# Nearest-neighbour upsampling: a first block of rows with its own partition layout, and a first store that waits for the second load

## The chip, the cores and the metric

The kernel runs on one core of a Trainium2 chip. Its engines run side by side and meet through semaphores: here VectorE (DVE in the profile) and ScalarE (ACT) copy within the on-chip memory, and SyncE (SP) issues the transfers, which 16 DMA engines carry out. The on-chip memory has 128 partitions. The metric is the device time of one execution in microseconds; the median of the runs counts.

## The reference

```python
def setup_inputs():
    batch, channels, h, w = (16, 64, 64, 64)
    return {'x': np.random.randn(batch, channels, h, w).astype(np.float32), 'scale_factor': 2}

def reference(x, scale_factor):
    batch, channels, h, w = x.shape
    new_h, new_w = (h * scale_factor, w * scale_factor)
    result = np.zeros((batch, channels, new_h, new_w), dtype=np.float32)
    for i in range(new_h):
        for j in range(new_w):
            result[:, :, i, j] = x[:, :, i // scale_factor, j // scale_factor].copy()
    return result.astype(np.float32)
```

Every element of x becomes a 2 x 2 square of the output. x has 65,536 rows of 64 floats (16.8 MB); each row becomes two output rows of 128 floats, 1 KB together (67.1 MB in all). Nothing is calculated: the kernel moves data.

## The kernel before

**Layout.** All rows of x are numbered through, and partition p owns rows 512p to 512p + 511 (`xp`, `op`). So a transfer of rows lo to hi takes one contiguous piece of memory per partition; the pieces of neighbouring partitions are 128 KiB apart in x and 512 KiB apart in the output.

**On-chip memory.** One tile `mem` holds, per partition, `FREE` = 79 rows' worth of output space (`WF` floats) and behind it all 512 rows of x (`xt`). An expanded chunk is written there too: chunks with an even number at offset 0, those with an odd number ending just below the first row of x that is still unread (line 208), so they lie partly over rows of x that are used up. Two chunks in a row never overlap, and every chunk overlaps the one before last. A copy into a chunk's place therefore waits until the store of the chunk before last has been read out and landed.

**Loads.** Three, cut at rows 0, 32, 288 and 512 (lines 192 to 195). All three are issued on SP one after the other, ahead of the barrier at the program's start (`begin_before_barrier` moves SP's first three instructions there; it needs them to have no waits).

**Chunks.** The loop at line 204 goes over nine chunks of `rows`. In each, VectorE expands the first `kv` rows (line 213) and ScalarE the others (line 214): the operand `expanded` reads each element twice for the columns and each row twice. In the first chunk ScalarE has one row only, in the others VectorE has 9/16. When both are done, SP issues the chunk's store (line 215). SP works in order: a store that waits holds all later ones back. All transfers share SP's one DMA queue.

**The end.** `close_early` arranges the waits and the clearing of semaphores behind the last store.

Of the kernel before, what the change touches and what calls it, by code (L numbers as in the profile page):

```python
# [153 lines left out]
@with_exitstack  # L154
def kernel(
    ctx: ExitStack,
    tc: tile.TileContext,
    x: bass.AP,
    scale_factor: int,
    out: bass.AP,  # L160
):
    nc = tc.nc
    nc.at_finalize(begin_before_barrier)
    nc.at_finalize(close_early)
    P = nc.NUM_PARTITIONS
    s = int(scale_factor)
    B, C, H, W = x.shape
    R = B * C * H // P
    fdt = x.dtype

    xp = x.rearrange("b c h w -> (b c h) w").rearrange("(p r) w -> p r w", p=P)
    op = out.rearrange("b c (h hd) w -> (b c h) (hd w)", hd=s).rearrange(
        "(p r) w -> p r w", p=P
    )

    rows = [54, 38, 52, 63, 52, 64, 63, 63, 63]
    GROW = s * s
    FREE = 79
    WF = FREE * GROW * W
    assert sum(rows) == R
    mem_pool = ctx.enter_context(tc.tile_pool(name="mem", bufs=1))
    mem = mem_pool.tile([P, WF + R * W], fdt, name="mem")
    xt = mem[:, WF:].rearrange("p (r w) -> p r w", r=R)

    HEAD = 32
    cuts = [0, HEAD, R // 2 + HEAD, R]
    for lo, hi in zip(cuts, cuts[1:]):
        nc.sync.dma_start(out=xt[:, lo:hi], in_=xp[:, lo:hi])  # L195

    def expanded(r0, r1):
        return (
            xt[:, r0:r1].unsqueeze(2).unsqueeze(4).to_broadcast([P, r1 - r0, s, W, s])
        )  # L200

    r0 = 0
    before = (0, 0)
    for n, k in enumerate(rows):
        size = k * GROW * W
        at = 0 if n % 2 == 0 else WF + r0 * W - size
        assert at >= before[1] or at + size <= before[0]
        before = (at, at + size)
        u = mem[:, at : at + size].rearrange(
            "p (k a w b) -> p k a w b", k=k, a=s, w=W  # L210
        )
        kv = k - 1 if n == 0 else k * 9 // 16
        nc.vector.tensor_copy(out=u[:, :kv], in_=expanded(r0, r0 + kv))  # L213
        nc.scalar.copy(out=u[:, kv:], in_=expanded(r0 + kv, r0 + k))  # L214
        nc.sync.dma_start(out=op[:, r0 : r0 + k, :], in_=u)  # L215
        r0 += k


# [33 lines left out]
```

## Time and profile before

| | |
|---|---|
| time, median of 3 runs | 197.24 us (196.97 to 197.29) |
| the profiled execution's own span | 195.86 us |
| VectorE busy | 78.6 us, 40% |
| ScalarE busy | 46.5 us, 24% |
| bytes moved | 83.89 MB, 428 GB/s over the span |
| DMA packets | 1728: for each of 12 transfers one per partition, and 16 for the semaphore |
| loads land (slowest engine) | 4.76, 24.10, 41.04 us |
| first store issued, landed | 38.57, 57.37 us |
| last store issued, landed | 167.3, 195.83 us |

The span goes from the first to the last instruction of the profiled execution; what lies around it, 1.38 us against the median, is the start and the end of the program. Times in the text are microseconds from the start of the span. A transfer is told by three moments: its issue on SP, the start and end of its packets on each DMA engine, and its landing, when the last of the 16 engines has raised the semaphore. In the groups of instructions, 128x8960 stands for 128 partitions with 8960 elements each: one row of x is 256 output elements, so that is 35 rows.

### The profile page before, as it was taken

What the parts mean: (1) busy time and instruction counts of PE and PEld (TensorE: products, weight loads), DVE (VectorE), ACT (ScalarE), POOL (GpSimd) and SP (SyncE); (2) the same over time, 40 slices, a digit from 0 to 9 for tenths busy, and PEclk for the clock granted to TensorE, in tenths of its full rate; (3) what the DMA queues carried; (4) which work ended last, traced back from release to release, by engine and by line L of the source; (5) the groups of instructions that cost most, each with busy time, mean ns of one, the idle gap of its engine ahead of it and who ended that gap; (6) DMA issues with size and microseconds to landing.
All of it is one profiled execution on the core that took longest, in us unless ns stands there. A gap on an engine that the chain in (4) does not pass through costs nothing.

```text
span 195.9 us, 102 instructions
## 1 busy us (share of the span) xinstructions
DVE 78.6 (40%) x9; ACT 46.5 (24%) x10; POOL 0.2 (0%) x4
## 2 busy tenths in 40 slices
DVE  0000099990029399078008106930692079100000
ACT  2000000160027093074910006665000074000000
POOL 0000000000000000000000000000000000000000
DMA  9999989889899989899999899999999999999994
GB/s 428 428 428 428 402 375 550 386 361 542 361 435 397 540 348 522 348 422 422 448 417 500 370 500 428 428 428 428 422 422 422 435 435 514 461 435 448 435 422 211
DMA packets 1728, 83.89 MB, mean 428 GB/s; under 512 B 192, under 2 KB 192, under 8 KB 192
## 3 DMA queue, kind: packets, MB, share of 16 engines
q1 hardware_dynamic: 1728, 83.89, 99.2%
HBM read 16.78 MB, written 67.11 MB: 428 GB/s over the span
## 4 chain that ended last, share of the span: by engine, by line
DMA 60%; DVE 25%; issue 0%; SPq 0%; DVEq 0%
DMA out_dram<-mem 48%; DVE mem L213 25%; DMA mem<-in_x_dram 12%; SPq L195 0%; DVEq L213 0%; SPq L215 0%
## 5 line engine op out<-in xcount | busy, mean ns | idle before, releaser
L213 DVE COPY mem<-mem 128x8960 f32<-128x8960 f32 (+4 forms) x9 | 78.6, 8745 | 88.7 <-DMA out_dram<-mem 64.5
L214 ACT COPY mem<-mem 128x7168 f32<-128x7168 f32 (+3 forms) x9 | 45.2, 5027 | 115.6 <-DMA out_dram<-mem 74.1
L214 ACT ACT_TABLE_LOAD x1 | 1.3, 1283 | 1.7 <-PEq L233 1.7
L233 POOL MEMSET const-uint8-127<- 128x1 uint8 x1 | 0.1, 102 | 0.0
L233 POOL MEMSET const-bfloat16-1.0<- 128x1 bf16 x1 | 0.1, 101 | 0.0
L233 POOL MEMSET const-float32-0.0<- 128x1 f32 x1 | 0.1, 98 | 0.2 <-issue 0.2
L233 POOL MEMSET const-float32-1.0<- 128x1 f32 x1 | 0.1, 98 | 0.0
## 6 DMA issues: line engine op xcount, KB each, us to landing
out_dram<-mem SPq DMA_DIRECT2D x4, 8064.0 KB, 28.5
out_dram<-mem SPq DMA_DIRECT2D x2, 6656.0 KB, 22.9
mem<-in_x_dram SPq DMA_DIRECT2D x1, 7168.0 KB, 40.1
out_dram<-mem SPq DMA_DIRECT2D x1, 6912.0 KB, 18.8
out_dram<-mem SPq DMA_DIRECT2D x1, 4864.0 KB, 24.7
mem<-in_x_dram SPq DMA_DIRECT2D x1, 1024.0 KB, 4.8
mem<-in_x_dram SPq DMA_DIRECT2D x1, 23.7
out_dram<-mem SPq DMA_DIRECT2D x1, 30.0
```

What stands on the lines that cost most here:

```text
L213: nc.vector.tensor_copy(out=u[:, :kv], in_=expanded(r0, r0 + kv))
L214: nc.scalar.copy(out=u[:, kv:], in_=expanded(r0 + kv, r0 + k))
L233: nc = _bacc.Bacc("TRN2", target_bir_lowering=False, num_devices=1)
```

## The change

The rows of x are dealt out in two blocks. Of the first 128 x 61 rows, partition p owns rows 61p to 61p + 60; of the remaining 128 x 451, it owns 451 consecutive ones. `of_partitions` gives the piece of x or of the output that holds rows lo to hi of every partition. The pieces of neighbouring partitions are now 15.25 KiB apart in the first load and 61 KiB in the first store, 112.75 and 451 KiB in the others.

The loads are cut at rows 0, 61, 480 and 512. The first load is what the first store needs; the last has 32 rows, 8 KB per partition. The chunks are 61, 33, 52, 63, 52, 63, 63, 63 and 62 rows (before: 54, 38, 52, 63, 52, 64, 63, 63, 63). VectorE's part of each chunk but the first falls from 9/16 to 7/16. The first store gets a wait for the second load's semaphore, besides the waits for its two copies.

```diff
-    xp = x.rearrange("b c h w -> (b c h) w").rearrange("(p r) w -> p r w", p=P)
-    op = out.rearrange("b c (h hd) w -> (b c h) (hd w)", hd=s).rearrange(
-        "(p r) w -> p r w", p=P
-    )
-    rows = [54, 38, 52, 63, 52, 64, 63, 63, 63]
+    FIRST = 61
+    xr = x.rearrange("b c h w -> (b c h) w")
+    orow = out.rearrange("b c (h hd) w -> (b c h) (hd w)", hd=s)
+    blocks = ((0, FIRST), (FIRST, R))
+
+    def of_partitions(t, lo, hi):
+        b0, b1 = next(b for b in blocks if b[0] <= lo and hi <= b[1])
+        whole = t[P * b0 : P * b1].rearrange("(p r) w -> p r w", p=P)
+        return whole[:, lo - b0 : hi - b0]
+
+    rows = [61, 33, 52, 63, 52, 63, 63, 63, 62]
...
-    HEAD = 32
-    cuts = [0, HEAD, R // 2 + HEAD, R]
-    for lo, hi in zip(cuts, cuts[1:]):
-        nc.sync.dma_start(out=xt[:, lo:hi], in_=xp[:, lo:hi])
+    cuts = [0, FIRST, R - 32, R]
+    loads = [
+        nc.sync.dma_start(out=xt[:, lo:hi], in_=of_partitions(xr, lo, hi))
+        for lo, hi in zip(cuts, cuts[1:])
+    ]
...
-        kv = k - 1 if n == 0 else k * 9 // 16
+        kv = k - 1 if n == 0 else k * 7 // 16
         nc.vector.tensor_copy(out=u[:, :kv], in_=expanded(r0, r0 + kv))
         nc.scalar.copy(out=u[:, kv:], in_=expanded(r0 + kv, r0 + k))
-        nc.sync.dma_start(out=op[:, r0 : r0 + k, :], in_=u)
+        store = nc.sync.dma_start(out=of_partitions(orow, r0, r0 + k), in_=u)
+        if n == 0:
+            tc.add_manual_dep(
+                store.ins,
+                loads[1].ins.name,
+                mybir.DependencyInfo(
+                    mybir.DependencyClass.Sync, mybir.DependencyReason.DATA
+                ),
+                reason="the first store goes behind the second load",
+            )
         r0 += k
```

## The prediction

> **What bounds the kernel now.** I read the page first, for which resource is full.
>
> ```profile
> span 195.9 us, 102 instructions
> ...
> DVE 0000099990029399078008106930692079100000
> ...
> DMA  9999989889899989899999899999999999999994
> ...
> q1 hardware_dynamic: 1728, 83.89, 99.2%
> ```
>
> The DMA engines are busy for 99.2% of the span, VectorE for 40%. 0.8% of 195.86 us is 1.6 us: that is all that lies outside packets. Next I read the chain of waits, to see where the copies touch the end.
>
> ```profile
> 0.43 23.67 DMA mem<-in_x_dram
> ...
> 24.20 14.30 DVE mem L213
> ...
> 38.57 18.80 DMA out_dram<-mem
> ...
> 57.46 7.90 DVE mem L213
> ...
> 65.43 19.09 DMA out_dram<-mem
> ```
>
> The chain alternates between copies and transfers, but this is only the order in which buffers come free: while a copy of the chain runs, the queue still has another transfer. So a faster copy gains nothing until the queue runs dry, and a slower one costs only from there. How near that is, the packet records of the trace (start, duration, size of each) show. Within an engine a packet normally starts 6 ns after the one before. The only gaps in the middle of the run are at the first store: it is issued at 38.57, the loads' packets end between 40.05 and 40.65 on the different engines, and three engines that ended at 40.21 to 40.24 got their first store packet only at 40.33 to 40.36. These three waited 0.13 us each; the slowest engine, which sets the end, did not wait.
>
> Third, the stretches, for the rate.
>
> ```profile
> 1.00:2.00 1.00, 0.00 (x0) 0.27 (x1) 0.00 (x0) 1.00 1.04 238
> 2.00:3.00 1.00, 0.00 (x0) 1.00 (x1) 0.00 (x0) 1.00 0.98 410
> 5.00:10.00 5.00, 0.00 (x0) 0.00 (x0) 0.00 (x0) 1.00 0.97 419
> 60.00:190.00 130.00, 56.14 (x7) 38.41 (x7) 0.00 (x0) 1.00 1.00 432
> ```
>
> The last column is GB/s, a packet's bytes counted at its end. Loads alone and stores alone run at the same rate; only the first microsecond of data is slow. The packet records agree: 64 KB load and store packets together take 2418.7 ns, 63 KB store packets 2381.4, 38 KB ones 1440.4. The line through the first and the last of these is 37.63 ns per KB and 10.6 ns per packet. One partition-row of a store (1 KB, eight partitions per engine) is thus 0.302 us and of a load 0.076: 512 rows are 154.8 and 38.7 us, 193.5 in all. The rest of the span is 1.01 us from the first issue to the first packet, 0.50 us per engine of slow first packets (29 of the 128 packets of 8 KB are over 320 ns where the others take 309), 0.36 us from the last packet to its landing, and engines that are 0.6 us apart from the first load on (they landed it at 4.16 to 4.76, and the last store at 195.08 to 195.83).
>
> **The change part by part.** Bytes stay, so 193.5 us stay.
>
> *Loads.* Three as before, issued in the same places, of 61, 419 and 32 rows. The second holds 419 x 256 = 107,264 bytes per partition, and no packet of this trace exceeds 65,536. Cut in two it makes 8 packets more per engine: 8 x 10.6 ns = +0.085 us on the path. Bounds: nothing if it stays whole; many small pieces is a rival. The Trainium skill, "DMA: Bandwidth & Descriptors", section "Why a DMA increments its semaphore by 16 and not by 1", implies that a contiguous row over 64 KiB must be cut and becomes many tiny pieces only where no divisor fits; 26,816 floats halve, which by that rule is the +0.085. No run here shows such a row yet.
>
> *The start.* The first packets are 15.25 KB instead of 8 and 15.25 KB apart in memory instead of 128. Bounds: the 0.50 us of slow packets goes (-0.50), or doubles with the packets' size (+0.50). I take -0.1: the slow packets all end before 2.7 us, as if it were a matter of time and not of bytes, and the rate at the end is that of the slowest engine, whose start (spread over 1.01 to 1.40) stays.
>
> *First copy.* It needs the first load alone: 29 rows more than before, 4.76 + 29 x 0.076 = landed at 7.0. VectorE has 60 rows. Among the nine VectorE groups one stands out:
>
> ```profile
> L213 DVE COPY mem<-mem 128x8960 f32<-128x8960 f32 x4 | 37.9, 9486 | 33.9 <-DMA out_dram<-mem 33.9
> L213 DVE COPY mem<-mem 128x13568 f32<-128x13568 f32 x1 | 14.3, 14286 | 24.2 <-DMA mem<-in_x_dram 24.2
> L213 DVE COPY mem<-mem 128x9216 f32<-128x9216 f32 x1 | 5.0, 4961 | 11.1 <-DMA out_dram<-mem 11.1
> L214 ACT COPY mem<-mem 128x7168 f32<-128x7168 f32 x5 | 30.8, 6165 | 56.1 <-DMA out_dram<-mem 49.7 <-DVE mem L213 6.4
> L214 ACT COPY mem<-mem 128x256 f32<-128x256 f32 x1 | 0.4, 405 | 21.1 <-DMA mem<-in_x_dram 21.1
> ```
>
> 36 rows (9216 elements) take 0.54 ns per element, all others, of an odd number of rows, 1.05. So 60 rows are 8.3 us by the even row, 16.2 by the odd: done at 15 to 23, hidden by the loads either way, with 15 us of cover.
>
> *The hold.* The first store waits on SP for the second load. The loads end as before plus 0.085. The last one is 8 packets x 309 ns + 9 ns for the semaphore = 2.48 us per engine, so the second lands at 41.04 (the loads' last landing) - 2.48 + 0.085 = 38.65, and 0.07 later (copy end 38.50 to issue 38.57 now) the store is issued: 38.72 against 38.57. From issue to the end of the loads on the slowest engine it is 40.65 + 0.085 - 38.72 = 2.02 us, now 2.08. The three late engines show 1.76 to 1.79 us from issue to a first store packet. So the slowest engine keeps 0.2 us, while the engines ahead wait some 0.1 to 0.3 us, which they have. Cost on the path 0; bounds 0 and 0.06 (if the slowest engine now has no slack). If the last load gave no cover at all: 0.36 + 0.07 + 1.79 = 2.2 us. Behind the held store on SP are only the other stores, and the next one's copies cannot begin before the second load either. Without the hold the store would queue behind all loads, so holding it moves no packet forward.
>
> *Second store.* 33 rows, 14 on VectorE, 19 on ScalarE. ScalarE's two rows above give 0.833 ns per element and 0.19 us: 4864 elements are 4.2 us, issue at 43.0, behind a first store that lasts until 59.
>
> *Third store.* It waits for the first store's buffer: landing at 57.37 + 7 rows x 0.302 + 0.085 = 59.6. ScalarE's 30 rows are 6.6 us, issue at 66.3, first packet by 68.1. The second store's 33 rows keep the fastest engine until 59.6 - 0.96 (landing delay and spread) + 10.0 = 68.6. Cover left 0.5 us on the fastest engine, 1.1 on the slowest; now it is 0.6 on the fastest (65.43 + 1.79 against 67.85). If ScalarE took over 1.1 us longer, the excess would count.
>
> *Later copies.* At 7/16, 27 rows on VectorE are 7.4 us, 36 on ScalarE 7.9, against 9.5 now. Each runs beside a store of 16 to 19 us: 0.
>
> **Sum:** +0.085 - 0.1 + 0 = 0 within 0.1. The profiled execution is 195.86, the median 197.24, 1.38 outside the span, and nothing of that is touched. Forecast 197.2 us.
>
> **Rivals.**
> *Strides cost time (faster).* The slow first microsecond would be 16 streams starting at addresses a power of two apart, and the new strides end it. For: 238 GB/s against 419, and the slow packets die out as the engines drift apart. Against: the same strides cost nothing later. Worth: the slowest engine landed its first load at 4.76; straight through it would be 1.01 + 8 x 0.309 + 0.34 = 3.82, so up to 0.9; two thirds of it, 0.6: 196.6. The Trainium skill, same page, section "Latency and other measured facts", says copies with a row pitch of 512 KiB ran at 207 GB/s per direction instead of 214. By that the stores, now at this pitch, would gain 3.3% of 154.8 = 5 us (192, an estimate). The trace speaks against it in that size: 37.8 ns per KB at both pitches, 128 and 512 KiB.
> *The held store comes late (slower).* Where: the end of the loads. It decides once the store's issue slips more than 0.2 us beyond 38.72, or its first packets need over 2.0 us; each microsecond beyond is one on the path, because the queue holds nothing else. For: three engines run dry already. Price between 0.4 and 2.2 us; 0.7 as the middle of the lower half: 197.9.
> *The new strides are worse (slower).* Output rows begin at any multiple of 1 KB instead of 512 KiB. Nothing in the trace speaks for it; each per cent on the stores is 1.5 us: 198.8.
> *The long load goes in 256-byte pieces (slower).* 3352 per engine at 9.4 + 10.6 ns are 67 us instead of 31.7: 232.
>
> **How the numbers follow.** A difference under 0.2% (0.39 us, 196.85 to 197.63) can't be told from none. No change 0.55 (0.03 of it below the bound, 0.02 above; own range 196.8 to 197.7), strides at the start 0.17 and in the page's size 0.02, held store late 0.15, worse strides 0.08, small pieces 0.03. Faster 0.03 + 0.17 + 0.02 = 0.22; slower 0.02 + 0.15 + 0.08 + 0.03 = 0.28; same 0.50. The range 196.5 to 198.4 leaves out the tails of the two stride cases and the dearer half of the late store, some 0.19.
>
> **What would show it.** 1856 packets (two pieces) and a DMA share of 99% confirm the sum. The first load landing at 7.0 confirms the start; under 6.4, the first rival. The hold is right if the first store is issued near 38.7 and the page's DMA row shows no dip near 40 us; a gap over 0.3 us there is the second rival. Store packets over 2390 ns for 63 KB show the third. The first copy taking 8 or 16 us must not move the end. The forecast is wrong if the slowest engine has a gap anywhere past the start, or if the rate of the stores changes.

## The result, and the profile after

The changed kernel takes 198.06 us (median of 5 runs, 197.92 to 198.15) against 197.24 us before (196.97 to 197.42): ratio 1.0042, 95% interval 1.003 to 1.0055. That is 0.8 us slower; no change to speak of, 197.2, was forecast, with a range that holds 198.06.

The profiled execution's span is 196.59 us against 195.86, so 0.73 of the 0.82 us is inside it. First the page of the changed kernel:

```profile
span 196.6 us, 99 instructions
...
DVE  0492000030006077051006804900590068000000
...
DMA  8999999799999998999999999999999999999994
...
q1 hardware_dynamic: 1856, 83.89, 99.2%
```

The DMA engines are still busy for 99.2%: 195.0 us of a span of 196.59, before 194.3 of 195.86. The same bytes kept the engines busy longer. A share of 99% says only that some packet was always open, not that it moved at full speed. The 1856 packets are the 128 more that were predicted. VectorE fell from 40% to 27% busy, and that bought nothing.

The chain of waits (start, duration, what):

```profile
0.43 38.78 DMA mem<-in_x_dram
...
39.30 20.83 DMA out_dram<-mem
...
60.16 6.60 ACT mem L220
...
66.78 19.02 DMA out_dram<-mem
```

It now runs through the second load (landed at 39.21) and the held store (issued at 39.30, 38.57 before). The prediction had 38.65 and 38.72. Why the load lands late shows in the stretches (from, to, length, three engines' busy time, clock, DMA share, GB/s):

```profile
1.00:2.00 1.00, 0.00 (x0) 0.22 (x1) 0.00 (x0) 1.00 1.33 250
2.00:3.00 1.00, 0.00 (x0) 1.00 (x1) 0.00 (x0) 1.00 0.76 281
3.00:4.00 1.00, 0.00 (x0) 0.06 (x1) 0.00 (x0) 1.00 1.02 437
```

Before, the second row read 410 GB/s: the start then was slow for one microsecond, now it is for two. The groups of instructions (busy time, mean ns of one, idle time before) show the first copy:

```profile
L219 DVE COPY mem<-mem 128x15360 f32<-128x15360 f32 x1 | 8.2, 8160 | 7.6 <-DMA mem<-in_x_dram 7.6
```

60 rows take 8.16 us, the fast rate of the even row. The copy begins at 7.61 and is done 23 us before its store may go.

The next table is from the packet records and landings of the two profiled executions, per engine on average where not said otherwise. The records do not name the engine, but within an engine a packet starts 3 to 4 ns before the recorded end of the one before, and so they can be put in line.

| | before | after | difference |
|---|---|---|---|
| first load's packets, over their plain length | 0.50 us | 0.85 us | +0.35 |
| 72 store packets, over their plain length | 0.11 us | 0.46 us | +0.36 |
| eight packets more | | | +0.08 |
| slowest engine behind the median one when the first load lands | 0.31 us | 0.61 us | |
| wait for the first store packet | 0.02 us | 0.12 us | +0.09 |
| engines that wait for it | 3 | 15 | |

"Plain" is the length that nearly all packets of a size have in the quietest runs: 2380 ns for a store packet of 63 rows. The first three differences add up, but for 0.04, to the 0.75 us that the engines are busy longer. They don't prove a cause: the time is that of the engine that ends last, and another engine can lose some without harm. The runs decide. The engine that lands the first load last is called the straggler below.

Where many engines wait at once, the records don't tell which of them waits how long: taken in order of time, the waits are 0.12 to 0.14 us before and 0.06 to 0.17 us after. The 0.77 us of one engine, of which the next section speaks, is the longest that any pairing allows.

### The profile page after: what moved, and what is told of

It is laid out like the page before. It is cut to its first block, busy times and chain, and to the rows that moved or that the text cites. A ratio compares the mean times of both kernels' runs of the same rounds, so it can differ in the third digit from the quotient of the medians.

```text
span 196.6 us, 99 instructions
## 1 busy us (share of the span) xinstructions
DVE 53.1 (27%) x9; ACT 58.3 (30%) x10; POOL 0.2 (0%) x4
## 2 busy tenths in 40 slices
DMA packets 1856, 83.89 MB, mean 427 GB/s; under 512 B 192, under 2 KB 192, under 8 KB 192
## 3 DMA queue, kind: packets, MB, share of 16 engines
q1 hardware_dynamic: 1856, 83.89, 99.2%
## 4 chain that ended last, share of the span: by engine, by line
DMA 70%; ACT 15%; SPq 0%; issue 0%
DMA out_dram<-mem 50%; DMA mem<-in_x_dram 20%; ACT mem L220 15%; SPq L199 0%; SPq L221 0%
## 5 line engine op out<-in xcount | busy, mean ns | idle before, releaser
L220 ACT COPY mem<-mem 128x9216 f32<-128x9216 f32 (+4 forms) x9 | 57.0, 6331 | 106.4 <-DMA out_dram<-mem 70.5
L219 DVE COPY mem<-mem 128x6912 f32<-128x6912 f32 (+3 forms) x9 | 53.1, 5905 | 113.0 <-DMA out_dram<-mem 82.0
```

## The experiments

All ratios are to the kernel before on the same chip. Two theories at first. *The deal* of the rows costs: the odd strides lengthen the store packets and slow the start. *The hold* costs: engines wait at the first store, single ones perhaps up to 0.77 us.

**Without the hold** (e1_no_hold)

```diff
-            tc.add_manual_dep(store.ins, loads[1].ins.name, ...)
```

> The changed kernel without the wait of the first store for the second load. If the deal of the rows is what costs (slow first packets 0.845 us per engine against 0.50, store packets 5 ns longer each, 8 packets more), the time stays at 198.0 us (ratio to the kernel before 1.003 to 1.005). If the hold is what costs (gaps of up to 0.77 us at the first store on single engines), it falls by 0.4 to 0.8 us to 197.3 to 197.6, and the gaps are gone from the packet records.

Measured: 199.56 us against 197.41 for the kernel before on that chip, ratio 1.0106 (1.0088 to 1.0124). Neither theory had that: the hold is worth about 1.3 us. The first store is issued at 16.14 here, some 25 us before the loads end, and still the loads suffer:

```profile
36.00:38.00 2.00, 0.00 (x0) 0.00 (x0) 0.00 (x0) 1.00 0.99 429
38.00:40.00 2.00, 0.50 (x1) 0.42 (x1) 0.00 (x0) 1.00 1.02 311
```

The packet records say it sharper. All 8 KB packets of the last load take 309 ns in the changed kernel; here about half of them take longer, up to 1,030, 0.9 us per engine together. The long second load ahead of them is untouched. And every store packet now has its plain length, in spite of the new strides (0.005 us over, instead of 0.46).

**The old deal, all else as changed** (e2_old_deal)

```diff
-    blocks = ((0, FIRST), (FIRST, R))
+    blocks = ((0, R),)
```

> The changed kernel with the old deal of the rows (512 consecutive rows per partition); chunk sizes, loads, hold and shares of the engines as changed. If the deal costs: the typical 63-row store packet is back at 2380 ns (now 2385), that is -0.36 us, and if the first packets are slow because of the deal too, their loss is back at 0.5 us, -0.35: 197.3 to 197.4. If the first packets are slow because they are twice as long, only -0.36: 197.7. If the hold costs: still 198.0.

Measured: 197.55, ratio 1.0007 (0.9998 to 1.0015). The deal carries nearly all of the loss; chunk sizes, the shares of the engines, the hold and the eight packets together cost at most 0.15%. The typical 63-row packet is back at 2380 ns; six engines wait for the held store, issued at 38.70, and have long store packets (0.20 us per engine on average). The loss of the first packets is 0.65 us, between the two values that were expected. How much of it is length and how much the deal one profile can't tell: profiles with the same first load differ by up to 0.18.

**Another deal alone, in the kernel before** (e3_deal_alone)

```diff
-    xp, op: 512 rows per partition
+    two blocks, of 259 and 253 rows per partition
-    cuts = [0, HEAD, R // 2 + HEAD, R]
+    cuts = [0, HEAD, 259, R]
```

> The kernel before with a deal of the rows in two blocks of 259 and 253 rows per partition as its only change (the second load ends at row 259 instead of 288, so no row exceeds 64 KB; the first load keeps 32 rows; no hold). If odd strides lengthen store packets: 5 ns on each of 72 packets per engine, +0.36 us, 197.6; if they also slow the first packets, up to +0.35 more, 197.9. If the hold or the long first packets cost: 197.2 as before.

Measured: 198.26, ratio 1.0046 (1.0033 to 1.0059), but not for either reason: the store packets are plain (2380 ns) at these odd strides and the first packets lose 0.47 us. The loss is in the last load, whose last packets are 1.2 us longer per engine. Stretches of this run:

```profile
36.00:38.00 2.00, 2.00 (x2) 1.72 (x1) 0.00 (x0) 1.00 1.01 291
38.00:40.00 2.00, 2.00 (x1) 2.00 (x1) 0.00 (x0) 1.00 0.79 227
40.00:42.00 2.00, 1.86 (x1) 0.10 (x1) 0.00 (x0) 1.00 1.03 442
```

The shorter second load had moved the first store's issue from 38.57 to 36.28, so I had changed two things. It is the early store again.

**A first load of 61 rows, in the kernel before** (e4_head61)

```diff
-    HEAD = 32
+    HEAD = 61
```

> The kernel before with a first load of 61 rows instead of 32 as its only change, so first packets of 15.25 KB with the old strides, and a first store that can be issued at 22 us, behind the loads, without a hold. If the length of the first packets sets their loss: 0.85 us instead of 0.50, 197.6. If the strides do: 0.5, 197.2. If an early issue of the first store disturbs the loads, their last landing moves beyond 41.4.

Measured: 198.29, ratio 1.0050 (1.0038 to 1.0062). The third outcome: store issued at 21.48, last loads landed at 42.31 instead of 41.04, the last load packets 1.2 us longer per engine. The first packets lose 0.64 us, neither of the two values that were expected.

From these four a *two-sided* theory: how the first store meets the end of the loads decides. Queued long ahead, it costs about 1.2 us on the last load packets (the switch). Late, the engine runs dry, and its later store packets stay some 6 ns long, to the end. In the changed kernel all engines but the straggler show the latter.

**Last load of 40 rows** (e6_last40), **of 24** (e7_last24) **and of 52** (e12_last52), in the changed kernel: `R - 32` in the cuts becomes `R - 40`, `R - 24`, `R - 52`.

> The changed kernel with a last load of 40 rows instead of 32, so that the hold ends 0.6 us earlier before the loads' end. Two-sided theory (an engine that has run dry before its first store packet pays some 6 ns on each later packet, 72 of them, 0.4 us; an engine whose store is queued long before its loads end pays 1.2 us on its last load packets; in between it pays neither): first store issued near 38.7, few engines dry, the typical 63-row store packet back at 2380 ns, 197.6 to 197.7 us. If the deal of the rows lengthens the store packets: still 2385 and 198.0.

> The changed kernel with a last load of 24 rows instead of 32, so that the hold ends 0.6 us later against the loads' end. Two-sided theory: all 16 engines dry, gaps 0.6 us longer, store packets still 6 ns long: 198.6 to 198.7 us. If the hold costs nothing on the path: 198.0.

> The changed kernel with a last load of 52 rows instead of 32: the hold ends some 1.5 us earlier against the loads' end, enough that a straggler in the first load doesn't let the others run dry. Two-sided theory: typical 63-row store packet at 2380 ns on all engines, a part of the switch cost instead (0.1 to 0.5 us on the last load packets), slow start kept (0.85 to 1.03): 197.7 to 198.0 us. If the deal of the rows lengthens the store packets: 2385 ns and 198.0 to 198.3.

Measured: 198.16 with 40 rows (ratio 1.0040, 1.0028 to 1.0053), 198.72 with 24 (1.0068, 1.0054 to 1.0082), 198.78 with 52 (1.0066, 1.0053 to 1.0078). 24 rows came within 0.02 us of what was expected (all but one engine ran dry, one for 1.09 us). 40 didn't: in its profile one engine landed the first load 0.99 us after the median one, and the hold, which waits for the slowest engine, ended as late as ever (store issued at 39.25). 52 rows did end most of the long store packets (0.12 us over, instead of 0.46), but the time rose above both values that were expected: one engine lands its last load at 42.82, the next slowest at 41.45, the median at 41.15. That engine was behind from the start, so for it the store was queued 4.3 us early, and it paid the most of the switch (one of its last load packets is 0.75 us over its plain length; five other engines lost 0.03 to 0.28 us). With a straggler no place for the hold is right for all engines.

**The first copy's shares, in the kernel before**: 51 rows on VectorE (e8_share51) and 52 (e9_share52).

```diff
-        kv = k - 1 if n == 0 else k * 9 // 16
+        kv = k - 3 if n == 0 else k * 9 // 16    # e9_share52: k - 2
```

> The kernel before with 51 rows of the first chunk on VectorE and 3 on ScalarE instead of 53 and 1: the first store is issued at 38.0 instead of 38.57. Two-sided theory: no engine is dry at the first store, the late packets of all engines have their plain length (now those of four engines are 2 to 6 ns longer, and these end last): 196.9 to 197.1 us, ratio 0.998 to 0.9995. If the moment of the first store does not matter: 197.3, ratio 1.000.

> The kernel before with 52 rows of the first chunk on VectorE and 2 on ScalarE: an even number of rows, so the copy takes 7 us instead of 14.3 and the first store is issued near 31.3, 9 us ahead of the loads' end. Two-sided theory: the last load packets of each engine are 1.2 us longer in all, later packets plain: 198.1 to 198.4 us. If an early issue is harmless: 197.0 to 197.3.

Measured: 197.41, ratio 1.0007 (0.9998 to 1.0015), and 198.50, ratio 1.0062 (1.0049 to 1.0074). The second is the cleanest test of the switch: one row moved between two copies that aren't the limit. Its timeline (start, duration; the first line holds the first two copies of VectorE):

```profile
24.41 12.75 DVE L213 COPY mem<-mem 128x13312 f32<-128x13312 f32 x2 [24.41 <-DMA mem<-in_x_dram]
31.59 3.82 ACT L214 COPY mem<-mem 128x4352 f32<-128x4352 f32 x1 [6.63 <-DVE mem L213]
31.59 5.99 SPq L215 DMA_DIRECT2D out_dram<-mem  x2
```

A copy that is 7 us faster makes the kernel 1.2 us slower, because its store is issued at 31.59; the last load packets are 1.04 us longer per engine. With 51 rows the store is issued at 38.22 (38.0 was expected; the second load landed 0.2 us later than in the profile before). No engine runs dry and the store packets are plain, as expected, but 0.13 us of the switch is paid already, and this execution's first packets lost 0.61. No gain can be told: the kernel before stands close to the best place.

**The border of the blocks at row 261** (e10_wide_first), in the changed kernel

```diff
-EARLY = 3
+EARLY = 4
...
-    blocks = ((0, FIRST), (FIRST, R))
+    blocks = ((0, 261), (261, R))
-    cuts = [0, FIRST, R - 32, R]
+    cuts = [0, FIRST, 261, R - 32, R]
...
-                loads[1].ins.name,
+                loads[2].ins.name,
```

> The changed kernel with the border of the two blocks moved from row 61 to row 261, and the second load cut there (four loads; 200 and 219 rows instead of one of 419 in two pieces, so as many packets; the first store waits for the third). The first load has 61 rows as in the changed kernel, but its pieces lie 65.25 KB apart instead of 15.25; no stride is a power of two. If the tight packing of the first load makes the start slow: loss of the first packets 0.65 us per engine (as with the old deal; 0.85 to 1.03 in four runs with the tight one), fewer engines dry, 197.5 to 197.7 us. If any odd stride does: 198.0.

Measured: 197.51 against 197.43, ratio 1.0005 (0.9997 to 1.0014). The first load is as long as in the changed kernel, no stride is a power of two, the hold and the number of data packets are the same, and the loss is gone. Its start, and in its chain of waits the load and the store that is held for it:

```profile
1.00:2.00 1.00, 0.00 (x0) 0.00 (x0) 0.00 (x0) 1.00 1.14 281
2.00:3.00 1.00, 0.00 (x0) 0.75 (x1) 0.00 (x0) 1.00 1.03 437
```

```profile
0.89 37.79 DMA mem<-in_x_dram
...
38.77 20.84 DMA out_dram<-mem
```

437 GB/s in the third microsecond, where the changed kernel had 281; first packets lose 0.51 us, the slowest engine is 0.35 behind the median, and the held store is issued at 38.77 instead of 39.30. So it is the tight first block. The border also pulls the pieces of the first store apart, from 61 to 261 KiB; but in the run without the hold (e1_no_hold) all 128 packets of the tight first store have their plain 2305 ns, so it is the load that counts. Eleven engines still wait at the first store, and the store packets are still 0.38 us over their plain length: by themselves they don't make the loss.

**A tight first block alone, in the kernel before** (e13_tight_alone)

```diff
+    two blocks, of 54 and 458 rows per partition
-    cuts = [0, HEAD, R // 2 + HEAD, R]
+    cuts = [0, 54, 310, R]
```

> The kernel before with a tight first block alone: two blocks of 54 and 458 rows per partition, loads of 54, 256 and 202 rows, no hold, chunks and shares as before. The first store is issued near 22 us, as in the kernel before with a first load of 61 rows and the old deal (ratio 1.0050). If the tight first load makes the start slow and leaves one engine behind wherever it stands: loss of the first packets 0.85 to 1.03 us per engine, slowest engine 0.6 to 1.0 us behind the median at the first load's landing, time 0.4 to 0.9 us above that kernel, ratio 1.007 to 1.0095. If the tight block harms only together with the hold: 1.005 and a loss of 0.65.

Measured: 199.25, ratio 1.0097 (1.008 to 1.0114). The tight block harms without the hold too. The mean loss of the first packets was only 0.59, not 0.85: what counts is the straggler, 0.89 us behind the median at the first landing, which ends last here. The start again:

```profile
2.00:3.00 1.00, 0.00 (x0) 1.00 (x1) 0.00 (x0) 1.00 0.78 290
```

**The old deal with loads of 220, 256 and 36 rows** (e11_even_loads), all else as changed

```diff
-    blocks = ((0, FIRST), (FIRST, R))
+    blocks = ((0, R),)
-    cuts = [0, FIRST, R - 32, R]
+    cuts = [0, R - 292, R - 36, R]
```

> The changed kernel with the old deal and loads of 220, 256 and 36 rows: as few packets as the kernel before, first packets of 55 KB, hold behind the second load with 36 rows to go. Two-sided theory: no or few engines dry, no early store, 0.085 us less than the old deal with 61, 419 and 32 rows (197.55). With the loss of the first packets between 0.5 and 0.9 us: 197.2 to 197.6. Below 197.1 it would beat both kernels.

Measured: 197.15 against 197.43, ratio 0.9992 (0.9983 to 1.0001). No engine is dry at the first store, the store packets are plain, 0.16 us of the switch is paid. It is the fastest of all, clearly faster than the changed kernel, but from the kernel before it can't be told apart.

The start in all profiles, by the first load (loss of its packets per engine; slowest engine behind the median when it lands):

| first load, distance of its pieces | profiles | loss, us | behind, us |
|---|---|---|---|
| 8 KB, 64.75 or 128 KiB apart | 4 | 0.47 to 0.61 | 0.20 to 0.36 |
| 15.25 KB, 65.25 or 128 KiB apart | 3 | 0.51 to 0.65 | 0.27 to 0.36 |
| 55 KB, 128 KiB apart | 1 | 0.59 | 0.22 |
| 15.25 KB, 15.25 KiB apart | 5 | 0.85 to 1.03 | 0.61 to 0.99 |
| 13.5 KB, 13.5 KiB apart | 1 | 0.59 | 0.89 |

## Why the prediction was wrong, point by point

*The start* is the step that failed first: "I take -0.1", of bounds -0.50 and +0.50. It measured +0.35 us per engine on average. On the straggler the first load landed at 7.59; at the old pace it would have been 4.76 + 29 x 0.076 = 6.96 (an estimate), so it came 0.63 late. The bounds took in the size of the packets; that packing the pieces tightly could be worse than a power of two was not weighed: the only rival on strides at the start ran the other way. The sign of that rival is refuted. Moving the border takes the change's 0.42% to 0.05%, so the tight first block accounts for some 0.7 of the 0.8 us.

The Trainium skill, "DMA: Bandwidth & Descriptors", section "Latency and other measured facts", advises padding a row pitch that is a large power of two, or laying tiles out contiguously; it measured copies between HBM tensors. Here the old pitches, 128 KiB for loads and 512 KiB for stores, cost nothing (store packets of 63 rows take 2380 ns and load packets of 64 KB 2418 ns at these and at odd ones), and the contiguous block made the start worse. The measurement decides for this kernel.

Followed to the end of the two profiled executions ("long" is what an engine's 72 store packets take over their plain length; us):

| engine | first store packet | long | stores end |
|---|---|---|---|
| before, the last of those that did not wait | 40.65 | 0 | 195.24 |
| before, the three that waited | 40.33 to 40.35 | 0.52 | 195.44 to 195.46 |
| changed, the straggler, which did not wait | 41.33 | 0 | 195.92 |
| changed, the last two of those that waited | 41.11, 41.13 | 0.50, 0.48 | 196.20 |

The rest, from an engine's first store packet to its end, is 154.59 us of plain packets in each row; where packets of two engines start within a few ns of each other, their lengths tell which is whose. Between the engines that did not wait lie 0.68 us: the 0.63 of the first load and 0.05 of the eight packets more. A delay from the start stays, as a saturated queue has nothing to catch up with. But neither profile ends with these engines. It ends with engines that waited, whose long packets carry them past, by 0.22 us before and by 0.28 after. Together this is 0.74 us, the difference of the spans. In e6_last40 and e13_tight_alone the straggler itself ends last.

*The hold, priced at 0 on the path (bounds 0 and 0.06)*, came out at these 0.06, though not as worked out. One input was wrong: the landing of the second load, 39.21 instead of 38.65, is the straggler's. With it the issue of the store, 39.30, passed the limit of the rival "the held store comes late" (0.2 beyond 38.72) by 0.38 us. Yet the waits did not grow by as much: in order of time they are 0.06 to 0.17 us, at or below the 0.1 to 0.3 that the working gave the engines ahead. "Which they have" is what failed: a wait costs an engine some 0.5 us more in long packets, in the kernel before too, and no term of the sum has that. It changes the time by little because three engines paid it before.

*"Holding it moves no packet forward"* is refuted. Without the hold the kernel loses another 0.64%, 1.3 us. Three runs of the kernel before with an early first store (e3_deal_alone, e4_head61, e9_share52) show the same switch, 1.0 to 1.2 us on the last load packets.

*What held:* the eight packets more (1856 on the page, and the old deal, which has them too, stays within 0.15% of before). On the path they are some 0.05 us instead of 0.085: packets do not start 6 ns behind the one before, as the prediction reads, but 3 to 4 ns ahead of its recorded end, so the 10.6 ns per packet shrink to some 7 from start to start (an estimate from packets of 54 and 64 KB, which follow each other at 2038.0 and 2414.1 ns). What held further: the copies at no cost in the changed kernel; the first copy at the even row's rate; the second and third stores' cover (no engine waits past the first store); the rate of the stores apart from the 6 ns. *The rival "new strides are worse"* on the stores falls: they are plain at odd strides when no engine ran dry.

The range held the time because the late store and the worse strides had been allowed for. That it did is luck: 198.06 came from a slow start, which no rival had, and the late store's 197.9, so near to it, was worked out for another cause. The chance of 0.50 on no change was too high for a sum whose least known term, the start, stood at ±0.5 us against a limit of 0.39.

## What to carry to other kernels

In a kernel that is one saturated queue, look at the slowest of the DMA engines, not at their mean share: a delay on one of them in the first three microseconds stays to the end. Don't pack the first load's pieces tightly because it looks tidy; compare the start's GB/s. Where loads give way to stores on one queue, when the first store is issued matters in both directions: in the kernel before, 2.3 us earlier cost 0.46% (e3_deal_alone); in the changed one, 1.1 us later left an engine idle for 1.09 us (e7_last24). A copy that isn't the limit can be what keeps that time.

## What the runs showed of the hardware that was not expected

- A store queued well before the loads end lengthens the last load packets by 0.9 to 1.4 us per engine (five runs, the store issued some 5 to 26 us before the loads ended), though it stands behind them in the queue. Issued 1.5 to 2.1 us ahead, as before, it costs nothing; 2.2 to 2.8 us ahead (e8_share51) it costs 0.13 us. Why is open.
- An engine that has run dry before its first store packet, be it for 0.1 us, keeps store packets 5 to 7 ns longer than plain (2386 for 2380 ns) to the end of the run, some 0.5 us in all; one that hasn't starts with plain ones. In the changed kernel's profile 15 of 16 engines have long ones, and the straggler has plain ones. In 14 profiles the sum over an engine's 72 store packets was between 0.005 and 0.50 us on average, following the number of dry engines, with one exception: in e12_last52 no engine waits at the first store, some turn long later, and the average is 0.12 us. Why is open.
- A first load whose pieces lie end to end starts slowly and leaves one to three engines 0.6 to 1.0 us behind; the same pieces 65 KiB or more apart don't. The cause (which memory or path the engines share) is open: only two tight layouts were tried, and no distance between 15 and 64 KiB.
